# A two-block transformer step on one core: forget-gate weights on VectorE, last outputs in turn, final scaling on two engines

## The chip, the cores and the metric

The kernel runs on one core of a Trainium2 chip. A core has TensorE (PE, matrix products), VectorE (DVE), ScalarE (ACT), GpSimd (POOL) and the queues that issue transfers, here SP's. The metric is the device time of one execution in microseconds (us), lower is better.

## The reference, cut to what matters

The reference sends one sequence of 256 tokens of width 1024 through two blocks. Three places matter here. In the second block's mixer, half of the heads are forgetting attention: a per-head gate, summed along the sequence, is added to the scores.

```python
log_f = jax.nn.log_sigmoid((f_logit + b_forget)).transpose(0, 2, 1)
c = jnp.cumsum(log_f, axis=-1)
s = einsum('bhqd,bhkd->bhqk', qi, k) * scale + cq[..., None] - c[:, :, None, :]
```

The second block ends with a layer of 16,384 small experts. For each token some experts get a gate, all others none; the output is the gated gelu of the token with the experts' first matrix, times their second matrix, and a last norm follows.

```python
a = gates * jax.nn.gelu(xt @ u.T)      # gates are zero but for the chosen experts
h = h + a @ v
out = h * lax.rsqrt(jnp.mean(h * h, axis=-1, keepdims=True) + 1e-6) * norm_final_g
```

## The kernel before

Every weight comes from memory in units of 128x1024 (512 KB). `unit` splits a unit into a high part (`whi`, ScalarE, line 206) and a low part (`wlo`, DVE, line 209, or POOL for a share of the columns that `pool_k` sets, line 211). A product is three matmuls: high by high, low by high, high by low (`mm3`, lines 231 to 233). `take` and `wtile` hand out units and make up to two ahead.

Work that is not the main stream of products is written as generators. `spawn(gen, rate)` puts one on a list; `tick(w)` adds rate x w to each generator's account and calls it once for each whole number. `linear` makes two column tiles of 128 a group, and calls `tick(0.5)` behind each half of a group, so there are two half-ticks a group. `drain` runs what is left to its end. The instructions then stand on each engine's queue in an order that a scheduler derives from the program's order and from what is ready; each engine takes its queue in order.

The forget gate. `fox_c` makes the summed gate `u` for eight heads (8 partitions, 256 columns). `lh` (the tile `selh`, 8 heads x 256 columns, partitions 0 to 7 and 64 to 71) holds selectors which are multiplied by 8 u, so that a product with `rh` adds the gate to the scores. `fox_c` runs between two linears of the mixer. Behind it attention over the first half of the heads is spawned at rate 2.05 (`attention`, without gate: `scores` line 1360, `soft` lines 1369 to 1377, `turn` line 1383, `weigh`), and a linear of six groups follows; then `drain`, and the attention that reads `lh` (line 1364) is spawned.

The experts. `GT` holds 128x256 values for each of 128 rows of experts. A linear of 64 groups makes the products with the first matrix, and `evu` applies the gelu (lines 1446 to 1450). Meanwhile `wstep` builds the gates of four tokens a call from two comparisons (lines 1460, 1461) and a scaling (line 1463); the call after, `place` multiplies them out (eight matmuls, line 1470) and multiplies or copies them into all rows of `GT` that are done (lines 1473, 1475). The products with the second matrix start only with `GT` complete: for each pair `i` of rows, `split` makes `ah` and `al` (lines 332, 333), and 24 matmuls (line 1539) add to four accumulators `acc[t][c]`, two halves of 128 tokens by two blocks of 512 columns.

The tail (lines 1541 to 1554). Each accumulator is added to the residual, squared and summed on ScalarE, the root and reciprocal give a factor for each token, and one DVE instruction for each block multiplies by it and by the gain `gf`. Four transfers on SP's queue write the blocks.

Of the kernel before, what the change touches and what calls it, by code (L numbers as in the profile page):

```python
# [8 lines left out]
FT = mybir.dt.float32  # L9
# [4 lines left out]
AF = mybir.ActivationFunctionType  # L14
OP = mybir.AluOpType
# [3 lines left out]
P = 128  # L19
S = 256  # L20
# [142 lines left out]
class Kernel:  # L163
# [1162 lines left out]
    def fox_c(self, psum, pd, ps, r2):  # L1326
        nc = self.nc
        V, SC = nc.vector, nc.scalar
        t = lambda nm, shape: pd.tile(shape, FT, name=nm)
        z, u = t("fz", [8, S]), t("fu", [8, S])  # L1330
        V.tensor_tensor(z, ps[0:8, :], r2[0:8, :], op=OP.mult)
        V.tensor_scalar(z, z, self.v("b_forget")[0:8], None, op0=OP.add)
        SC.activation(u, z, AF.Abs)
        SC.activation(u, u, AF.Exp, scale=-1.0)
        SC.activation(u, u, AF.Ln, bias=1.0)
        V.tensor_scalar(z, z, 0.0, None, op0=OP.min)
        V.tensor_tensor(z, z, u, op=OP.subtract)
        V.tensor_tensor_scan(u, self.ones[0:8, 0:1].to_broadcast([8, S]), z, 0.0, op0=OP.mult, op1=OP.add)
        lh, rh, w = self.selh, t("frh", [P, S]), t("fw", [P, S])
        nc.gpsimd.memset(rh, 1.0)  # L1340
        for b in (0, 64):
            c = w[b:b + 8]
            V.tensor_scalar(c, u, 8.0, None, op0=OP.mult)
            nc.gpsimd.tensor_tensor(lh[b:b + 8], lh[b:b + 8], c[:, None, :].to_broadcast([8, 8, S]), op=OP.mult)
            V.tensor_scalar(rh[b + 32:b + 40, :], u, -8.0, None, op0=OP.mult)
        self.fox = (lh, rh)

    def attention(self, psum, pd, q, k, vt, amask, fox, oh, ol):
        nc = self.nc
# [60 lines left out]
    def peer(self):  # L1410
        nc, tc = self.nc, self.tc
        V, SC, G, T = nc.vector, nc.scalar, nc.gpsimd, nc.tensor
        x = self.xres
        with ExitStack() as es:
            pk = es.enter_context(tc.tile_pool(name="pk", bufs=1))
            it = {n: pk.tile([P, S], FT, name="t" + n) for n in ("i", "j", "g")}
            GT = pk.tile([P, P, S], FT, name="GT")
            with ExitStack() as e2:
# [36 lines left out]
                def build(t0):  # L1455
                    oj = pw.tile([P, 4, P], FT, name="oj")
                    om = pw.tile([P, 4, P], FT, name="om")
                    oe = wide[2 + t0 // 4 % 2].rearrange("p a (b c) -> p (a b) c", b=2)
                    z = slice(t0, t0 + 4)
                    V.tensor_tensor(oe, io4, it["i"][:, z, None].to_broadcast([P, 4, P]), op=OP.is_equal)  # L1460
                    V.tensor_tensor(oj, io4, it["j"][:, z, None].to_broadcast([P, 4, P]), op=OP.is_equal)
                    for j in range(4):
                        SC.activation(om[:, j, :], oe[:, j, :], AF.Copy, scale=it["g"][:, t0 + j:t0 + j + 1])  # L1463
                    return t0, oj, om

                def place(t0, oj, om):
                    i1 = st["u"]
                    wps = psum.tile([P, 4, P], FT, name="ax")
                    for j in range(4):
                        T.matmul(wps[:, j, :], oj[:, j, :], om[:, j, :], start=True, stop=True)  # L1470
                    z = slice(t0, t0 + 4)
                    if i1:
                        V.tensor_tensor(Gv[:, z, :i1], Gv[:, z, :i1], wps[:, :, :i1], op=OP.mult)
                    if i1 < P:
                        SC.activation(Gv[:, z, i1:], wps[:, :, i1:], AF.Copy)
                    st["n"] = t0 + 4

                def wstep():
                    q = []
                    for t0 in range(0, S, 4):  # L1480
                        if len(q) == 1:
                            place(*q.pop(0))
                        q.append(build(t0))
                        yield
                    for p in q:
                        place(*p)
                        yield

                def start_w():
                    for _ in top():  # L1490
                        yield
                    self.pool_k = 0
                    self.spawn(wstep(), 1.65)

                self.pool_k = 8

                def evq(n, ps):
                    SC.activation(qh[:, n:n + 2, :], ps, AF.Copy)
                    st["q"] = n + 2

                self.spawn(start_w(), 1.6, "top", pin=PIN)
                self.linear(psum, hh, hl, 16, 8, evq, outer=True)
                for k in range(0, 8, 2):
                    SC.activation(hh[:, k:k + 2, :], hn[:, k:k + 2, :], AF.Copy)
                    (G if k % 4 else V).tensor_tensor(hl[:, k:k + 2, :], hn[:, k:k + 2, :], hh[:, k:k + 2, :].bitcast(FT),  # L1505
                                                     op=OP.subtract)
# [6 lines left out]
                acc = [[psum.tile([P, 512], FT, name="ax") for _ in range(2)] for _ in range(2)]  # L1513
                pv = po
                flat = lambda k: GT[:, k:k + 8, :].rearrange("p a b -> p (a b)").rearrange("p (t d) -> p t d", t=2)
                xt, o, sq = flat(0), flat(8), flat(16)
                gf = GT[:, 24:28, :].rearrange("p a b -> p (a b)")

                def turn(t, c):
                    tp = psum.tile([P, 4, P], FT, name="ax")  # L1520
                    for k in range(4):
                        T.transpose(tp[:, k, :], x[:, 4 * c + k, t * P:(t + 1) * P], self.ident)
                    SC.activation(xt[:, t, c * 512:(c + 1) * 512], tp.rearrange("p a b -> p (a b)"), AF.Copy)

                for i in range(0, P, 2):
                    ah = pv.tile([P, 2, S], FR, name="ah")
                    al = pv.tile([P, 2, S], FR, name="al")
                    self.split(GT[:, i:i + 2, :], ah, al)
                    if i == 32:
                        nc.sync.dma_start(gf, self.A["gf"])  # L1530
                    if 32 < i <= 40:
                        turn(*divmod(i // 2 - 17, 2))
                    for u in range(2):
                        wh, wl = (w.rearrange("p a b -> p (a b)") for w in self.take(2))
                        for t in range(2):
                            z = slice(t * P, (t + 1) * P)
                            for n, (a, w) in enumerate(((ah, wh), (al, wh), (ah, wl))):
                                for c in range(2):
                                    T.matmul(acc[t][c], a[:, u, z], w[:, c * 512:(c + 1) * 512],  # L1539
                                             start=i + u == 0 and n == 0, stop=i + u == P - 1 and n == 2)  # L1540
                self.warm_sqrt(GT[:, P - 1, 0:1])
                ss = pv.tile([P, 2, 2], FT, name="ss")
                for t in range(2):
                    r = self.r1[:, t:t + 1]
                    for c in range(2):
                        z = slice(c * 512, (c + 1) * 512)
                        V.tensor_tensor(o[:, t, z], xt[:, t, z], acc[t][c], op=OP.add)
                        SC.activation(sq[:, t, z], o[:, t, z], AF.Square, accum_out=ss[:, t, c:c + 1])
                    V.tensor_tensor(r, ss[:, t, 0:1], ss[:, t, 1:2], op=OP.add)
                    self.rsqrt(r, r, 1.0 / D, 0)  # L1550
                    for c in range(2):
                        z = slice(c * 512, (c + 1) * 512)
                        V.scalar_tensor_tensor(o[:, t, z], o[:, t, z], r, gf[:, z], op0=OP.mult, op1=OP.mult)  # L1553
                        nc.sync.dma_start(self.out[:, t, z], o[:, t, z])

    def topk(self, psum, qh, keys, scr, it, st):
        nc = self.nc
# [124 lines left out]
```

## Time and profile before

| | |
|---|---|
| Median of 3 runs | 1574.6 us (1574.18 to 1577.16) |
| Time of the profiled execution | 1572.57 us |
| Its span, first to last instruction | 1570.8 us |
| Mean granted TensorE clock | 0.986 of full |
| Busy: PE, DVE, ACT, POOL | 1515.3, 1132.9, 837.0, 345.7 us |

The span is what the trace holds; the profiled execution's time is 1.8 us longer. Busy times are sums over stages with different limits.

### The profile page before, as it was taken

Reading aid. Unit: us, or ns where it says so; the run is one execution under the profiler, and the core shown is the slowest. Engines: PE = TensorE matmul, PEld = TensorE weight load, DVE = VectorE, ACT = ScalarE, POOL = GpSimd, SP = SyncE. Lnnn points to the kernel's source line nnn. Section 1 sums busy time; section 2 is a strip of 40 time slices with the busy share of each in tenths; the row PEclk is TensorE's granted clock in tenths of the full one; section 3 lists DMA queues with packets and bytes.
Section 4 is the critical chain, followed back from the end, with each engine's and each line's share of the span. In section 5 each row is a group of like instructions: output and inputs, shape, how many; then the busy total and the mean of one; then the engine's idle time right before and its main releaser. Section 6 shows DMA issues by size and latency. Waiting matters only on the chain.

```text
span 1570.8 us, 28981 instructions
## 1 busy us (share of the span) xinstructions
PE 1515.3 (96%) x11494; PEld 1412.3 (90%) x11494; DVE 1132.9 (72%) x1801; ACT 837.0 (53%) x1399; POOL 345.7 (22%) x303
## 2 busy tenths in 40 slices
PE   6898999999999989999999999999999999999997
PEld 5897889999999989999999999999998888888886
DVE  8789975887645676667688967888997555555554
ACT  4563334756644455545455457777765445444543
POOL 7514644335400120025791600000000000000000
PEclk9899999999999999999999999999999999999999
DMA  9455457476565644546555554444454666666663
GB/s 365 155 156 168 162 181 223 147 255 202 178 188 185 195 128 135 148 148 219 158 175 189 162 188 147 149 141 155 137 157 151 194 207 187 191 195 193 193 196 121
DMA packets 75448, 279.67 MB, mean 178 GB/s; under 512 B 8368, under 2 KB 9008, under 8 KB 73648
## 3 DMA queue, kind: packets, MB, share of 16 engines
q1 hardware_dynamic: 75312, 277.82, 55.9%
q8 instruction: 90, 1.47, 0.4%
q14 instruction: 46, 0.38, 0.1%
HBM read 275.69 MB, written 2.10 MB: 177 GB/s over the span
## 4 chain that ended last, share of the span: by engine, by line
PE 46%; DVE 2%; POOL 1%; issue 1%; ACT 0%; DVEq 0%; ACTq 0%
PE ax L1539 22%; PE mm L233 7%; PE mm L232 7%; PE mm L231 7%; PE ax L1470 4%; POOL wlo L211 1%; POOL GT L1604 0%; DVE GT L1636 0%; DVE wlo L209 0%; DVE GT L1634 0%; PE ax L1577 0%; DVE GT L1553 0%; ACT whi L206 0%; DVE GT L1614 0%; DVE GT L1615 0%
## 5 line engine op out<-in xcount | busy, mean ns | idle before, releaser
L206 ACT ACTIVATE whi<-raw 128x1024 fp32r<-128x1024 f32 x453 | 478.9, 1058 | 549.7 <-PE mm L232 199.0
L209 DVE TENSOR_TENSOR wlo<-raw,whi 128x1024 fp32r<-128x1024 f32 (+2 forms) x413 | 496.6, 1204 | 267.0 <-ACT whi L206 266.3
L231 PE MATMUL mm<-hh,whi 128*128 128x256 f32 x1816 | 524.8, 289 | 3.7 <-ACT gate L581 2.5
L233 PE MATMUL mm<-hh,wlo 128*128 128x256 f32 x1816 | 515.5, 284 | 3.1 <-DVE wlo L209 2.3
L232 PE MATMUL mm<-hl,whi 128*128 128x256 f32 x1816 | 512.7, 282 | 1.1 <-DVE hl L1505 0.7
L231 PEld LDWEIGHTS mm<-hh,whi 128*128 128x128 f32 x1816 | 344.9, 190 | 10.3 <-issue 5.2
L233 PEld LDWEIGHTS mm<-hh,wlo 128*128 128x128 f32 x1816 | 345.5, 190 | 5.0 <-DVE wlo L209 2.7
L232 PEld LDWEIGHTS mm<-hl,whi 128*128 128x128 f32 x1816 | 346.2, 191 | 2.9 <-issue 1.4
L211 POOL TENSOR_TENSOR wlo<-raw,whi 128x256 fp32r<-128x256 f32 (+2 forms) x112 | 187.4, 1679 | 161.0 <-ACT whi L206 105.0
L1539 PE MATMUL ax<-whi,ah 128*128 128x512 f32 x512 | 158.7, 391 | 3.9 <-ACT ah L332 3.9
L1539 PE MATMUL ax<-whi,al 128*128 128x512 f32 x512 | 158.4, 391 | 0.0
L1539 PE MATMUL ax<-wlo,ah 128*128 128x512 f32 x512 | 158.2, 390 | 0.0
L1539 PEld LDWEIGHTS ax<-whi,ah 128*128 128x128 f32 x512 | 96.0, 188 | 23.9 <-ACT ah L332 4.1
L1539 PEld LDWEIGHTS ax<-whi,al 128*128 128x128 f32 x512 | 96.5, 189 | 20.4 <-DVE al L333 0.4
L1539 PEld LDWEIGHTS ax<-wlo,ah 128*128 128x128 f32 x512 | 96.5, 188 | 20.1
L1463 ACT ACTIVATE om<-xres,tg 128x128 f32<-128x128 f32 x256 | 84.9, 392 | 1.0 <-DVE xres L1460 1.0
L233 PE MATMUL ax<-hh,wlo 128*128 128x258 f32 x256 | 73.0, 285 | 1.7 <-DVE wlo L209 1.6
L231 PE MATMUL mm<-fh,whi 128*128 128x256 f32 x256 | 73.0, 285 | 0.0
L233 PE MATMUL mm<-fh,wlo 128*128 128x256 f32 x256 | 72.9, 285 | 0.0
L232 PE MATMUL mm<-fl,whi 128*128 128x256 f32 x256 | 72.9, 285 | 0.0
L231 PE MATMUL ax<-hh,whi 128*128 128x258 f32 x256 | 72.6, 284 | 0.0
L232 PE MATMUL ax<-hl,whi 128*128 128x258 f32 x256 | 72.2, 282 | 0.0
(531 smaller groups left out, 2377.6 us busy)
## 6 DMA issues: line engine op xcount, KB each, us to landing
raw<-in_wts SPq DMA_DIRECT2D x453, 512.0 KB, 3.6
raw<-in_ada SPq DMA_DIRECT2D x24, 512.0 KB, 4.2
araw<-in_ada SPq DMA_DIRECT2D x8, 1024.0 KB, 7.9
w0r<-in_w SPq DMA_DIRECT2D x8, 576.0 KB, 8.9
araw<-in_ada SPq DMA_DIRECT2D x8, 512.0 KB, 4.9
x<-in_x SPq DMA_DIRECT2D x1, 1024.0 KB, 5.0
mb<-in_x SPq DMA_DIRECT2D x2, 512.0 KB, 5.0
selh<-in_att SPq DMA_DIRECT2D x1, 1024.0 KB, 5.9
```

The source lines that it names most:

```text
L206: nc.scalar.activation(hi, raw, AF.Copy)
L209: nc.vector.tensor_tensor(lo[:, :c], raw[:, :c], hi[:, :c].bitcast(FT), op=OP.subtract)
L211: nc.gpsimd.tensor_tensor(lo[:, c:], raw[:, c:], hi[:, c:].bitcast(FT), op=OP.subtract)
L231: mm(ps, wh, xh, start=start, stop=False, **kw)
L232: mm(ps, wh, xl, start=False, stop=False, **kw)
L233: mm(ps, wl, xh, start=False, stop=stop, **kw)
L1463: SC.activation(om[:, j, :], oe[:, j, :], AF.Copy, scale=it["g"][:, t0 + j:t0 + j + 1])
L1470: T.matmul(wps[:, j, :], oj[:, j, :], om[:, j, :], start=True, stop=True)
L1539: T.matmul(acc[t][c], a[:, u, z], w[:, c * 512:(c + 1) * 512], start=i + u == 0 and n == 0, stop=i + u == P - 1 and n == 2)
```

## The change

Three edits. In `fox_c` the two POOL multiplies of 8x2048 elements become a generator of eight DVE multiplies of 8x512, spawned at rate 0.8. `wstep` is spawned at 1.75 in place of 1.65. At the end, the table load for the square root moves from behind the loop into pair 64; the last pair takes both its units first and ends the four accumulators one after another; the gain is multiplied in ahead of the factor, into a place of its own, and the factor is then applied by DVE for one block and by ScalarE for the other.

```diff
@@ fox_c @@
             V.tensor_scalar(c, u, 8.0, None, op0=OP.mult)
-            nc.gpsimd.tensor_tensor(lh[b:b + 8], lh[b:b + 8], c[:, None, :].to_broadcast([8, 8, S]), op=OP.mult)
             V.tensor_scalar(rh[b + 32:b + 40, :], u, -8.0, None, op0=OP.mult)
         self.fox = (lh, rh)
+
+        def weights():
+            for h in range(0, 8, 2):
+                yield
+                for b in (0, 64):
+                    z, c = lh[b:b + 8, h:h + 2], w[b:b + 8]
+                    V.tensor_tensor(z, z, c[:, None, :].to_broadcast([8, 2, S]), op=OP.mult)
+
+        self.spawn(weights(), 0.8)
@@ start_w @@
-                    self.spawn(wstep(), 1.65)
+                    self.spawn(wstep(), 1.75)
@@ the last loop @@
-                xt, o, sq = flat(0), flat(8), flat(16)
+                xt, o, sq, og = flat(0), flat(8), flat(16), flat(28)
...
+                    if i == 64:
+                        self.warm_sqrt(ah[:, 0, 0:1].bitcast(FT))
+                    if i < P - 2:
...
+                    else:
+                        us = [[w.rearrange("p a b -> p (a b)") for w in self.take(k)] for k in (1, 0)]
                         for t in range(2):
                             z = slice(t * P, (t + 1) * P)
-                            for n, (a, w) in enumerate(((ah, wh), (al, wh), (ah, wl))):
-                                for c in range(2):
-                                    T.matmul(acc[t][c], a[:, u, z], w[:, c * 512:(c + 1) * 512],
-                                             start=i + u == 0 and n == 0, stop=i + u == P - 1 and n == 2)
-                self.warm_sqrt(GT[:, P - 1, 0:1])
+                            for c in range(2):
+                                for u, (wh, wl) in enumerate(us):
+                                    for n, (a, w) in enumerate(((ah, wh), (al, wh), (ah, wl))):
+                                        T.matmul(acc[t][c], a[:, u, z], w[:, c * 512:(c + 1) * 512],
+                                                 start=False, stop=u == 1 and n == 2)
@@ the tail @@
                         V.tensor_tensor(o[:, t, z], xt[:, t, z], acc[t][c], op=OP.add)
                         SC.activation(sq[:, t, z], o[:, t, z], AF.Square, accum_out=ss[:, t, c:c + 1])
+                        V.tensor_tensor(og[:, t, z], o[:, t, z], gf[:, z], op=OP.mult)
...
-                        V.scalar_tensor_tensor(o[:, t, z], o[:, t, z], r, gf[:, z], op0=OP.mult, op1=OP.mult)
-                        nc.sync.dma_start(self.out[:, t, z], o[:, t, z])
+                        if c:
+                            SC.activation(og[:, t, z], og[:, t, z], AF.Copy, scale=r)
+                        else:
+                            V.tensor_scalar(og[:, t, z], og[:, t, z], r, None, op0=OP.mult)
+                        nc.sync.dma_start(self.out[:, t, z], og[:, t, z])
```

In all pairs but the last the 24 matmuls stay as they were.

## Rows read from the trace of the kernel before

**Rows 1.** TensorE's waits over the span: total, times, longest, in us.
```profile
PE ax L1383 <- DVE sc L1377: 5.6, 2, 4.2
...
PE ax L1539 <- ACT ah L332: 3.9, 1, 3.9
```

**Rows 2.** Busy time by stretch; (x) instructions; then granted clock, DMA share, GB/s.
```profile
580.00:600.00 20.00, 18.80 (x142) 17.90 (x143) 16.81 (x38) 11.99 (x29) 0.00 (x0) 0.86 0.54 158
...
880.00:900.00 20.00, 18.28 (x151) 17.79 (x150) 19.79 (x30) 10.55 (x13) 8.75 (x4) 1.00 0.51 160
...
1180.00:1200.00 20.00, 20.00 (x173) 20.00 (x173) 18.67 (x23) 13.91 (x36) 0.00 (x0) 1.00 0.53 156
1200.00:1220.00 20.00, 16.12 (x89) 13.74 (x88) 11.93 (x12) 9.04 (x15) 0.00 (x0) 0.91 0.49 160
...
1380.00:1400.00 20.00, 20.00 (x90) 16.57 (x89) 11.09 (x11) 9.73 (x12) 0.00 (x0) 1.00 0.64 197
```

**Rows 3.** Instructions in order of time, POOL and DVE: start, duration, idle before.
```profile
569.14 4.69 POOL L1344 TENSOR_TENSOR selh<-selh,fw 8x2048 f32<-8x2048 f32 x1 [18.70 <-DVE fw L1343]
574.13 4.53 POOL L1344 TENSOR_TENSOR selh<-selh,fw 8x2048 f32<-8x2048 f32 x1 [0.30 <-DVE fw L1343]
...
568.79 0.27 DVE L1343 TENSOR_SCALAR fw<-fu 8x256 f32<-8x256 f32 x1
...
569.39 4.59 DVE L1343 TENSOR_SCALAR fw<-fu 8x256 f32<-8x256 f32 x1
...
575.47 3.54 DVE L1377 TENSOR_SCALAR sc<-sc,mx 128x128 f32<-128x128 f32 x2
```

**Rows 4.** Instructions in order of time, TensorE, 573 to 595.
```profile
573.71 0.93 PE L1360 MATMUL ax<-ka,qa 64*128 64x128 f32 x8
578.80 0.95 PE L1383 MATMUL ax<-main,sc 128*128 128x128 f32 x3 [4.16 <-DVE sc L1377]
...
581.73 0.56 PE L231 MATMUL mm<-hh,whi 128*128 128x256 f32 x1
...
585.66 0.28 PE L231 MATMUL mm<-hh,whi 128*128 128x256 f32 x1
...
593.13 0.93 PE L1360 MATMUL ax<-ka,qa 64*128 64x128 f32 x8
...
594.62 0.36 PE L231 MATMUL mm<-hh,whi 128*128 128x256 f32 x1
```

**Rows 5.** Instructions in order of time, all engines, 1204 to 1215.
```profile
1204.78 1.05 PE L1470 MATMUL ax<-om,oj 128*128 128x128 f32 x8
...
1205.93 0.58 ACT L1449 ACTIVATE xres<-mm 128x504 f32<-128x504 f32 x1
...
1206.53 1.28 ACT L440 ACT_TABLE_LOAD   x1
...
1207.73 1.26 DVE L1473 TENSOR_TENSOR GT<-GT,ax 128x512 f32<-128x512 f32 x1
...
1209.71 0.80 PE L1539 MATMUL ax<-whi,ah 128*128 128x512 f32 x2 [3.88 <-ACT ah L332]
...
1214.30 0.62 PE L1539 MATMUL ax<-whi,ah 128*128 128x512 f32 x2
```

**Rows 6.** The chain that ended last, from 1540: start, time, what.
```profile
1539.83 21.77 PE ax L1539 x96
...
1561.63 0.70 DVE GT L1547
...
1562.35 1.33 ACT GT L1548 x4
...
1564.10 1.42 DVE GT L1553 x2
...
1565.63 0.75 DVE GT L1553
1566.38 0.66 DVEq L1677
```

More of the change, by code (lines that the diff above doesn't have):

```diff
@@ L1532, in peer @@
                         turn(*divmod(i // 2 - 17, 2))
-                    for u in range(2):
-                        wh, wl = (w.rearrange("p a b -> p (a b)") for w in self.take(2))
+                    if i == 64:
+                        self.warm_sqrt(ah[:, 0, 0:1].bitcast(FT))
+                    if i < P - 2:
+                        for u in range(2):
+                            wh, wl = (w.rearrange("p a b -> p (a b)") for w in self.take(2))
+                            for t in range(2):
+                                z = slice(t * P, (t + 1) * P)
+                                for n, (a, w) in enumerate(((ah, wh), (al, wh), (ah, wl))):
+                                    for c in range(2):
+                                        T.matmul(acc[t][c], a[:, u, z], w[:, c * 512:(c + 1) * 512],
+                                                 start=i + u == 0 and n == 0, stop=False)
+                    else:
+                        us = [[w.rearrange("p a b -> p (a b)") for w in self.take(k)] for k in (1, 0)]
                         for t in range(2):
                             z = slice(t * P, (t + 1) * P)
-                            for n, (a, w) in enumerate(((ah, wh), (al, wh), (ah, wl))):
-                                for c in range(2):
-                                    T.matmul(acc[t][c], a[:, u, z], w[:, c * 512:(c + 1) * 512],
-                                             start=i + u == 0 and n == 0, stop=i + u == P - 1 and n == 2)
-                self.warm_sqrt(GT[:, P - 1, 0:1])
+                            for c in range(2):
+                                for u, (wh, wl) in enumerate(us):
+                                    for n, (a, w) in enumerate(((ah, wh), (al, wh), (ah, wl))):
+                                        T.matmul(acc[t][c], a[:, u, z], w[:, c * 512:(c + 1) * 512],
+                                                 start=False, stop=u == 1 and n == 2)
                 ss = pv.tile([P, 2, 2], FT, name="ss")
```

## Prediction

> **What bounds the kernel now.** I read the stretches first (busy time of each engine in windows of 20 us), because the share over the whole span hides where TensorE is not the limit. In most of the second half TensorE is busy for 20.00 of 20 us with a granted clock of 1.00, as in 1180 to 1200 [rows 2]; there a change of another engine is worth nothing. Two windows fall out: 580 to 600 (18.80, clock 0.86) and 1200 to 1220 (16.12, clock 0.91) [rows 2]. The list of TensorE's waits names the same two places: line 1383 waits for line 1377 twice, 5.6 us together, and line 1539 waits once for line 332, 3.9 us [rows 1]. Then I read both places in order of time, and last the chain that ended last, for the tail. The change touches these three places, so the forecast is three terms.
>
> **Place one, the forget-gate weights.** Two POOL multiplies of 8x2048 elements run from 569.14 and 574.13, 4.69 and 4.53 us [rows 3]. In the same time a DVE tensor_scalar of 8x256 takes 4.59 us from 569.39 (to 573.98, when the first multiply has ended at 573.83), and two of line 1377 take 3.54 us from 575.47 (to 579.01, the second multiply ends at 578.66) [rows 3]. Both DVE instructions end about when POOL lets go, so I read them as held by POOL. TensorE is behind them: eight score matmuls start at 573.71, the transposes only at 578.80, after 4.16 us of idle time, and the next projection matmul at 581.73 [rows 4]. One cycle later the same two steps take 594.62 - 593.13 = 1.49 us [rows 4]; here 581.73 - 573.71 = 8.02, so 6.5 us are lost. Then 18 matmuls need 585.66 - 581.73 = 3.93 us [rows 4], 0.218 each, where 173 fit into 20.00 us of an undisturbed window, 0.116 each [rows 2]: about half rate, the lower of the two levels, after that idle time. That is 18 x 0.102 = 1.8 us more. Place one costs 8.3 us.
>
> The change takes both POOL multiplies away. DVE gets eight multiplies of 8x512 instead, by the nearest row, a DVE add of 512 columns, 0.70 us each [rows 6]: 5.6 us. They are issued late and apart: at 0.8 per tick and six ticks in that linear, the generator is called at half-ticks 3, 5 (or 6), 8 and 10; the first call only yields, three give a pair each (1.4 us), and the last pair falls into the drain. So no pair stands in front of the first softmax, which is what TensorE waited for. Behind a pair wait the next wlo subtraction and the softmax of a later cycle. DVE is idle for 3.19 us even of 580 to 600 [rows 2], which still holds work delayed by POOL. I cost the eight multiplies at nothing; without that idle time a pair would delay TensorE by its 1.4 us, three pairs by 4.2.
>
> What is late next at place one is the DVE work itself: without POOL, the held tensor_scalar gives back 4.59 less the 0.27 us of the same instruction before it, 4.3, and the pair of line 1377 gives back 3.54 less twice 0.27, 3.0, so 7.3 together, against 6.5 us that TensorE lost [rows 3, 4]. That leaves under 1 us of slack, so I keep 0.8 us of wait and take 7.5 us of 8.3 as saved; ends: 8.3, and 0 if the held DVE instructions had another cause.
>
> **Place two, the end of the expert stage.** wstep needs 65 calls (64 builds, and the last placement). At 1.65 a half-tick adds 0.825, so call 65 comes at half-tick 79; at 1.75 it adds 0.875 and call 65 comes at half-tick 75. The trace has the last eight placement matmuls at 1204.78, behind the last linear matmul [rows 5]: half-tick 79 is the last of the stage. The new last placement thus comes two groups earlier, inside the stream.
>
> Behind the old last placement stands a chain: its DVE multiply from 1207.73 for 1.26 us, then ah, then the first matmul of line 1539 at 1209.71, after 3.88 us of idle time [rows 5]. The next twelve matmuls need 1214.30 - 1209.71 = 4.59 us [rows 5]; the chain's last 96 need 21.77, 0.227 each [rows 6], so twelve should need 2.72: 1.9 us lost at the lower clock. Place two costs 5.8 us. The eight placement matmuls are only moved. With the placement done two groups earlier, the first two rows of GT are final and ah and al of the first pair can be made under the last groups. I take 5.3 us as saved, keeping 0.5 for whatever ScalarE still has in front of ah. From below: ah behind the last gelu (it ends at 1206.51 [rows 5]) plus about 0.7 for ah gives a first matmul at 1207.2, a saving of 2.5 with the clock lost all the same.
>
> The faster rate itself costs DVE nothing on the path, but its cover is thin. DVE is busy for 18.67 of 20 us in 1180 to 1200 [rows 2]; if all of it grew by 1.75/1.65 it would be 19.8. So DVE stays under TensorE, by 1% at least. If that cover is gone over the last nine groups, some 65 us, each per cent too much costs 0.65 us; I keep 0 to 2 us and take 0.
>
> **Moved table load.** warm_sqrt goes from behind the loop into pair 64. The trace has a load of 1.28 us, from 1206.53, before ah, which ends at 1207.81, while ah's input is ready only at 1207.73 + 1.26 = 1208.99 [rows 5]; so it binds nothing now. In the loop ScalarE is busy 9.73 of 20 us [rows 2], so in a pair of 24 x 0.227 = 5.4 us it is idle 2.8; the load and its one-column activation fit in. Cost 0. [...]
>
> **Place three, the tail.** The last matmul ends at 1561.60, the last scaling at 1567.04, 5.44 us later [rows 6]. The old chain: add 0.70, two squares in a row 1.33, root and reciprocal 0.41, then four scalings by line 1553 with a reciprocal between them, from 1564.10 on [rows 6]. With the accumulators ending in turn, a quarter of 24 x 0.227 = 1.36 us apart, only the last add and one square (0.67) follow the last matmul, then the sum (0.2, estimated as half of root and reciprocal, another one-column operation), root and reciprocal 0.41, and one scaling, on DVE and ScalarE side by side. For it the 0.75 us of the old one [rows 6] is the nearest row. Sum: 0.70 + 0.67 + 0.2 + 0.41 + 0.75 = 2.7; with the hand-overs of 0.02, 2.8. Saved: 2.6. The gain-weight multiply (0.70 again) of the last block lies beside its square; but that of the block before may stand ahead of the last add on DVE, and two output transfers now become ready together on SP's one queue. I take 2.0; ends 0.9 (both delays) and 2.7. Reading both units of the last pair at once wants the last wlo some 2 us earlier; TensorE has no wait anywhere in this loop but its first [rows 1], and units are made ahead. Cost 0.
>
> **Sum.** 7.5 + 5.3 + 2.0 = 14.8 us. The profiled execution took 1572.57 us (span 1570.8), so it would take 1557.8; the median of the runs shown is 2.0 us above that execution, 1574.6, so I forecast 1559.8 for the median.
>
> **Rivals.**
> 1. A new wait at place one: the softmax is late again because DVE's order puts other work before it (a wlo subtraction, or a weights pair). For it: under 1 us of slack. Against: the pairs are issued later. It leaves some 4 us of the wait and the low clock behind it, 5.5 in all: 1565.
> 2. At place two ah stands behind the gelu: saving 2.5 instead of 5.3, so 1562.6. For it: in the old order ah is ScalarE's last. Against: there it could not be earlier, its input was not ready.
> 3. Slower: DVE becomes the bound at 1.75. Place: 1100 to 1190, where its load is highest. If TensorE starved there and fell to the lower clock, a group of 48 matmuls would cost 48 x 0.102 = 4.9 us more, so three eat the gain of 14.8 and the point from which it decides is the fourth; five give 1559.8 + 24.5 = 1584. For it: the high DVE share. Against: the 1% of cover, and that 1.7 us of idle time in 880 to 900 left the clock at 1.00 [rows 2]. [...]
> 4. The change doesn't do what it says at place one: the held DVE instructions had another cause, and the wait stays. Then 5.3 + 2.0 are saved: 1567.3.
>
> **Chances and range.** Forecast 0.68, rival 1 0.10, rival 2 0.11, rival 3 0.04, rival 4 0.05, nothing at all 0.02. The likeliest's own range is 1557 to 1563.5: all gains at their upper ends (8.3 + 5.8 + 2.7 = 16.8) give 1557.8, less some spread of the runs (1574.18 to 1577.16). Taking in rivals 1 and 2 and most of rival 4: 1557 to 1567. By more than 0.2% (3.1 us, about what a measurement of this kernel can tell from no change) faster: all cases but rival 3 and nothing, 0.94; same 0.03; slower 0.03.
>
> **What would show it.** Right: no POOL work at 569 to 579, DVE's tensor_scalars of 8x256 at 0.3 us, TensorE at 20.00 with clock 1.00 where now 580 to 600 stands; no wait of line 1539 for ah at its start, the last placement two groups before it; from the last matmul to the last scaling 3.4 us in place of 5.44. Wrong: a wait of line 1383 for line 1377 that stays over 2 us; waits of line 1470 or 233 for DVE between 930 and 1200; the last add behind another DVE multiply by over 0.7 us.

## The result, and the profile after

The changed kernel took 1557.83 us (median of 4 runs, 1556.54 to 1561.31), the kernel before 1574.39 (median of 4, 1572.68 to 1577.16). The ratio is 0.9899, with a 95% interval of 0.9887 to 0.991: 1.0% faster, 16.6 us by the medians. The forecast was 1559.8 with a range of 1557 to 1567. The profiled execution took 1556.54 us with a span of 1554.8, against 1572.57 and 1570.8 before, so the profiled spans differ by 16.0 us.

To see where these 16.0 us come from, I cut both spans at the same five instructions: the first DVE operation on the forget gate (fz), the first score matmul that reads its weights, the first placement matmul of the expert stage, and the first and the last matmul of the last loop. The differences of start times in the trace, in us:

| stretch | before | after | difference | forecast |
|---|---|---|---|---|
| start to fz (untouched) | 560.95 | 560.45 | -0.50 | 0 |
| fz to first score matmul (place one) | 60.45 | 52.20 | -8.25 | -7.5 |
| to first placement matmul (untouched) | 310.67 | 310.55 | -0.12 | 0 |
| to first matmul of the last loop (place two, wait) | 277.64 | 273.60 | -4.04 | -3.4 |
| to its last matmul (place two, clock) | 351.72 | 349.84 | -1.88 | -1.9 |
| to the end (tail) | 9.33 | 8.13 | -1.20 | -2.0 |

All three places became shorter, the first two by more than was forecast, the tail by less; the untouched stretches moved by 0.5 us and 0.1. In the rows of stretches (columns as in [rows 2]) the two windows that had fallen out are full, and in the expert stage the window with the highest DVE share still leaves TensorE at 20.00:

```profile
580.00:600.00 20.00, 20.00 (x170) 18.18 (x169) 19.01 (x42) 12.44 (x31) 0.00 (x0) 1.00 0.51 157
...
1100.00:1120.00 20.00, 20.00 (x173) 20.00 (x173) 19.58 (x24) 14.60 (x38) 0.00 (x0) 1.00 0.43 133
...
1200.00:1220.00 20.00, 20.00 (x90) 16.57 (x89) 10.97 (x11) 9.85 (x12) 0.00 (x0) 1.00 0.79 249
```

TensorE is at 20.00 and the granted clock at 1.00 where [rows 2] had 18.80 and 0.86, and 16.12 and 0.91. Neither wait of [rows 1] is in the list of waits of the changed kernel.

**Place one.** DVE in order of time, the counterpart of [rows 3]:

```profile
568.88 0.28 DVE L1343 TENSOR_SCALAR fw<-fu 8x256 f32<-8x256 f32 x1
...
570.64 0.54 DVE L1385 TENSOR_SCALAR sc<-sc,mx 128x128 f32<-128x128 f32 x2
...
572.75 0.16 DVE L1383 RECIPROCAL mx<-mx 128x2 f32<-128x2 f32 x1
572.82 0.66 DVE L1352 TENSOR_TENSOR selh<-selh,fw 8x512 f32<-8x512 f32 x1
573.41 0.53 DVE L1385 TENSOR_SCALAR sc<-sc,mx 128x128 f32<-128x128 f32 x2
```

The second scaling of the gate takes 0.28 us in place of 4.59, the pair of softmax scalings 0.54 in place of 3.54. Yet the first weights multiply does not come late: it stands at 572.82, between the reciprocal and the scalings of the second softmax; in front of the first softmax's scalings (570.64) there is none, as forecast. TensorE, the counterpart of [rows 4], does not notice:

```profile
573.22 0.93 PE L1368 MATMUL ax<-ka,qa 64*128 64x128 f32 x8
574.08 0.88 PE L1391 MATMUL ax<-main,sc 128*128 128x128 f32 x6
574.71 0.36 PE L231 MATMUL mm<-hh,whi 128*128 128x256 f32 x1
```

From the score matmuls to the next projection it takes 574.71 - 573.22 = 1.49 us, the undisturbed step of [rows 4]. The second softmax is done at 573.94, and the six transposes start at 574.08, behind the score matmuls. As three belong to each softmax ([rows 4] has them in threes) and six take 574.71 - 574.08 = 0.63 us, the second softmax is needed, as an estimate, at 574.4: the multiply had some 0.4 us of room.

**Place two.** DVE, ScalarE and TensorE at the end of the expert stage, the counterpart of [rows 5]:

```profile
1187.45 1.32 DVE L1481 TENSOR_TENSOR GT<-GT,ax 128x496 f32<-128x496 f32 x1
...
1188.88 0.62 ACT L332 ACTIVATE ah<-GT 128x512 fp32r<-128x512 f32 x1
...
1192.19 0.58 ACT L1457 ACTIVATE xres<-mm 128x512 f32<-128x512 f32 x1
...
1196.68 0.28 PE L233 MATMUL mm<-hh,wlo 128*128 128x256 f32 x1
1196.80 0.63 PE L1550 MATMUL ax<-whi,ah 128*128 128x512 f32 x2
```

The last placement's multiply ends at 1188.77, 8.0 us ahead of the loop; ah is made in front of the last gelu, not behind it; the first matmul of the loop follows the last linear one without a gap.

**The tail.** DVE and ScalarE around the last add (line 1566), then the chain that ended last, the counterpart of [rows 6]:

```profile
1546.43 0.69 DVE L1568 TENSOR_TENSOR GT<-GT 128x512 f32<-128x512 f32 x1
1547.06 0.69 DVE L1566 TENSOR_TENSOR GT<-GT,ax 128x512 f32<-128x512 f32 x1
...
1548.39 0.48 DVE L1576 TENSOR_SCALAR GT<-GT,r 128x512 f32<-128x512 f32 x1
1548.41 0.71 ACT L1574 ACTIVATE GT<-GT,r 128x512 f32<-128x512 f32 x1
1548.79 0.15 DVE L1569 TENSOR_TENSOR r<-ss 128x1 f32<-128x1 f32 x1
...
1549.03 0.28 ACT L378 ACTIVATE r<-r,eps 128x1 f32<-128x1 f32 x1
```

```profile
1547.78 0.72 ACT GT L1567 x2
1548.51 0.61 ACT GT L1574
1549.12 0.19 ACT r L378
...
1549.53 0.72 ACT GT L1574
```

The last matmul starts at 1546.64, the last add 0.42 us behind it, as the gain multiply of the block before ends; the sum (1548.79), root, reciprocal and two scalings side by side follow. In front of the sum and the root stand the scalings of the first half of the tokens, on DVE (1548.39) and on ScalarE (1548.41). The last scaling ends at 1550.25: 3.6 us. Before, the same two were 1561.43 and 1567.04, 5.6 us. (The forecast's 5.44 counted from 1561.60, which in the trace is the end of the next-to-last matmul; from the end of the same matmul, 1546.80, it is 3.46 now.) So 2.0 us are saved up to there, but only 1.2 arrive at the end. The four output transfers of 256 KB, issued in pairs in the changed kernel and apart in the one before, show why. The time from issue to landing, for the changed kernel first, then for the kernel before, last for the last output of the kernel before alone:

```profile
L1577 SPq DMA_DIRECT2D out<-GT x4: 332/384/450, 1548.9 to 1550.4; - x4
...
DMA to landing us min/median/max: 2.4/2.9/3.2
```

```profile
L1554 SPq DMA_DIRECT2D out<-GT x4: 332/338/343, 1564.9 to 1567.1; - x4
...
DMA to landing us min/median/max: 2.4/2.5/2.7
```

```profile
L1554 SPq DMA_DIRECT2D out<-GT x1: 332/332/332, 1567.1 to 1567.1; - x1
...
DMA to landing us min/median/max: 2.5/2.5/2.5
```

The last output now leaves within 0.4 us of the third and lands 3.20 us after its issue; before, it left 0.7 us after the third and landed after 2.55. (The 2.7 of the kernel before is its second output's.) That is 0.65 us; another 0.14 is the last issue, which stands 0.17 us behind its scaling in place of 0.03. Together they are the 0.8 us that do not arrive.

### The profile page after: what moved, and what is told of

Read it like the earlier page. It is cut to its first block, busy times and chain, and to the rows that moved or that the text cites. A ratio compares the mean times of both kernels' runs of the same rounds, so it can differ in the third digit from the quotient of the medians.

```text
span 1554.8 us, 28988 instructions
## 1 busy us (share of the span) xinstructions
PE 1510.4 (97%) x11494; PEld 1409.9 (91%) x11494; DVE 1130.5 (73%) x1811; ACT 839.1 (54%) x1400; POOL 335.9 (22%) x301
## 4 chain that ended last, share of the span: by engine, by line
PE 46%; DVE 2%; POOL 1%; issue 1%; ACT 0%; DVEq 0%
PE ax L1550 22%; PE mm L233 7%; PE mm L232 7%; PE mm L231 7%; PE ax L1478 4%; POOL wlo L211 1%; POOL GT L1627 0%; DVE GT L1659 0%; DVE GT L1566 0%; DVE GT L1657 0%; DVE wlo L209 0%; PE ax L1600 0%; DVE GT L1568 0%; DVE GT L1637 0%; DVE GT L1638 0%
## 5 line engine op out<-in xcount | busy, mean ns | idle before, releaser
L209 DVE TENSOR_TENSOR wlo<-raw,whi 128x1024 fp32r<-128x1024 f32 (+2 forms) x413 | 496.3, 1204 | 265.0 <-ACT whi L206 264.4
L1481 DVE TENSOR_TENSOR GT<-GT,ax 128x208 f32<-128x208 f32 (+31 forms) x64 | 62.4, 974 | 16.1 <-PE ax L1478 15.9
```

Source lines behind the costliest of these rows:

```text
L209: nc.vector.tensor_tensor(lo[:, :c], raw[:, :c], hi[:, :c].bitcast(FT), op=OP.subtract)
```

## The experiments

### The three parts alone

`a_fox` has the kernel before with the forget-gate part only, `b_rate` with the rate only, `c_tail` with the edits of the last loop and the tail only.

```
a_fox   -   nc.gpsimd.tensor_tensor(lh[b:b + 8], lh[b:b + 8], c..., op=OP.mult)
        +   def weights(): ...
        +   self.spawn(weights(), 0.8)
b_rate  -   self.spawn(wstep(), 1.65)
        +   self.spawn(wstep(), 1.75)
c_tail  +   the last pair ordered by accumulator; og = o * gf; scaling on DVE and ACT; warm_sqrt at i == 64
```

> The kernel before with the forget-gate edit alone. Theory (three separate places, place one worth 8.3 us by its trace): span 1570.8 - 8.3 = 1562.5, no wait of the transposes for the softmax near 574, clock 1.00 in 560 to 620; the wait of 3.9 us at the start of the last loop and the lower clock behind it stay. Rival (the rate or the tail edit did part of it, or the gain at place one is given back at the end of the expert stage, whose call positions are unchanged): span above 1565.

> The kernel before with the rate 1.75 alone. Theory: place two is worth 5.8 to 6.0 us: span 1564.9, no wait of the first matmul of the last loop, last placement two groups before it. Rival (DVE, busier at this rate, makes TensorE wait before 1190, and the gain is smaller): waits of lines 233 or 1470 for DVE and a span above 1566.

> The kernel before with the edits of the last loop and the tail alone. Theory: from the last matmul to the last scaling 3.4 us in place of 5.4, but the last outputs land some 0.7 us later after their issue than before, so the span is 1.3 us shorter, 1569.5. Rival (the landing in the changed kernel was chance): span 2.0 us shorter or more, 1568.8.

| | median us | ratio to before, 95% | fz to scores | placements to loop | loop | tail |
|---|---|---|---|---|---|---|
| before | 1573.7 | | 60.5 | 277.6 | 351.7 | 9.3 |
| a_fox | 1566.78 | 0.9955 (0.9939 to 0.9972) | 52.2 | 277.6 | 351.5 | 9.3 |
| b_rate | 1570.7 | 0.9979 (0.9969 to 0.9988) | 60.8 | 273.6 | 349.8 | 9.3 |
| c_tail | 1572.71 | 0.9995 (0.9985 to 1.0005) | 60.3 | 277.6 | 351.6 | 8.2 |

In the stretches each part moves its own place, and the others behind fz by 0.4 us at most: -8.3, -5.9 (-4.0 and -1.9) and -1.2, which makes the 15.4 that the three places give in the whole change. The medians say less: 6.9 + 3.0 + 1.0 = 10.9, against 16.6 for the whole. In the profiled executions the difference lies ahead of every edit: fz begins at 564.0, 565.9 and 564.6 us in those of the three, at 560.9 and 560.5 in those of before and after. That the other executions lose their time in the same place is likely, but they have no trace. So the median of one part is no measure of its price here, and c_tail's alone is inconclusive; the stretches decide. For the same reason the spans that were expected of the three parts and of the next two runs are missed by 2.7 to 5.3 us; less the later begin of fz, all five come within 0.4 us of the value expected or into its range. All later stretches of this section are read in the same way.

### Is it POOL that holds DVE, or where the multiplies stand

`d_poolbg` leaves the eight multiplies in the background but gives them to POOL. `e_inline` leaves them on DVE but issues all eight at once, in front of the first softmax. Both are edits of the changed kernel.

```
d_poolbg  -   V.tensor_tensor(z, z, c[:, None, :]..., op=OP.mult)
          +   nc.gpsimd.tensor_tensor(z, z, c[:, None, :]..., op=OP.mult)
e_inline  -   self.spawn(weights(), 0.8)
          +   for _ in weights(): pass
```

> The changed kernel with the eight background multiplies on POOL in place of DVE. Theory (POOL's reads hold a DVE tensor_scalar until the running POOL instruction ends): POOL does them one after another from 569 on, some 1.2 us each; single DVE tensor_scalars are stretched by up to 1.2 us each but not by 4, so TensorE waits 0 to 3 us: span 1555 to 1558. Rival (the DVE instruction of before was slow by itself, not through POOL): no DVE instruction is stretched, span 1554.8 or less, as DVE has less to do.

> The changed kernel with the eight DVE multiplies issued at once in fox_c, not as a background part. Theory (what counts is what stands in front of the first softmax on DVE): 5 us of multiplies come ahead of it, TensorE waits 4 to 5 us for line 1386 (the softmax's scaling) near 574 and runs some matmuls at the lower clock: span 1554.8 + 4.5 to 6.5 = 1559.3 to 1561.3. Rival (the gain is only from leaving POOL, the background part is of no matter): span 1554.8 to 1555.5.

d_poolbg took 1563.31 us (ratio 0.9922, 0.9903 to 0.994), e_inline 1566.5 (0.9947, 0.9931 to 0.9964); from fz to the scores they need 54.7 and 58.4 us, 2.5 and 6.2 more than the changed kernel. So the move to DVE and the place in the background are each worth something. In d_poolbg POOL and DVE overlap; first POOL in order of time:

```profile
573.77 1.39 POOL L1352 TENSOR_TENSOR selh<-selh,fw 8x512 f32<-8x512 f32 x1 [18.69 <-DVE fw L1343]
575.45 12.26 POOL L1352 TENSOR_TENSOR selh<-selh,fw 8x512 f32<-8x512 f32 x7 [0.30 <-DVE fw L1343]
```

The multiplies by their line (duration in ns, shortest, median and longest), and DVE in the same stretch:

```profile
L1352 POOL TENSOR_TENSOR selh<-selh,fw x8: 1260/1400/2167, 573.8 to 585.5; 8x512 f32<-8x512 f32 x8
```

```profile
573.41 0.27 DVE L1343 TENSOR_SCALAR fw<-fu 8x256 f32<-8x256 f32 x1
...
574.02 1.29 DVE L1343 TENSOR_SCALAR fw<-fu 8x256 f32<-8x256 f32 x1
...
575.65 0.69 DVE L1278 TENSOR_TENSOR qb<-mm,r 128x512 f32<-128x512 f32 x1
...
576.79 1.57 DVE L1385 TENSOR_SCALAR sc<-sc,mx 128x128 f32<-128x128 f32 x2
...
578.80 1.82 DVE L209 TENSOR_TENSOR wlo<-raw,whi 128x1024 fp32r<-128x1024 f32 x1
...
582.02 2.30 DVE L209 TENSOR_TENSOR wlo<-raw,whi 128x1024 fp32r<-128x1024 f32 x1
```

The same gate scaling takes 0.27 us with POOL idle, 1.29 behind a POOL multiply that ends at 575.16 (the scaling ends 0.15 us later, at 575.31), and 4.59 behind the long one of [rows 3], where it ends 0.15 us later too. Its time follows the length of the POOL instruction (1.39 and 4.69 us), so I read it as held until POOL lets go; in both traces the POOL instruction had begun 0.25 us earlier. The pair of softmax scalings is held as well, for 1.57 us in place of 0.54. Not every DVE instruction is: the product of line 1278 takes 0.69 us with POOL at work, as it does without (0.69 in the changed kernel). Two wlo subtractions stretch too, from 1.22 to 1.82 and 2.30, and a POOL multiply takes up to 2.17 us where the shortest takes 1.26: both sides are longer there. What sets the instructions that are held apart from the one that is not, no run shows.

The two runs also show what becomes of the wait on TensorE. First d_poolbg, then e_inline (DVE, then TensorE):

```profile
581.99 0.61 PE L1391 MATMUL ax<-main,sc 128*128 128x128 f32 x3 [2.24 <-DVE sc L1385]
...
582.55 0.28 PE L232 MATMUL mm<-hl,whi 128*128 128x256 f32 x1
```

```profile
573.48 5.54 DVE L1352 TENSOR_TENSOR selh<-selh,fw 8x512 f32<-8x512 f32 x8
...
580.19 0.54 DVE L1386 TENSOR_SCALAR sc<-sc,mx 128x128 f32<-128x128 f32 x2
```

```profile
580.52 0.95 PE L1392 MATMUL ax<-main,sc 128*128 128x128 f32 x3 [2.42 <-DVE sc L1386]
...
581.48 0.41 PE L232 MATMUL mm<-hl,whi 128*128 128x256 f32 x1
...
583.03 0.41 PE L232 MATMUL mm<-hl,whi 128*128 128x256 f32 x1
```

In e_inline the eight multiplies take 5.54 us and push the softmax behind them: TensorE waits 2.42 us (4 to 5 were expected), and its matmuls then follow each other at 0.21 us, not 0.12, until 587.5. The granted clock of 580 to 600 is 0.83. In d_poolbg the wait is 2.24 us and the matmuls behind it keep 0.12; its clock is 1.00. The 6.2 us of e_inline are the 2.4 of wait, another 0.54 at 582.43, and some 30 matmuls that take 0.1 longer each at the lower clock. This is what rival 1 of the prediction describes.

A third try, `i_poolafter`, was to keep the two long POOL multiplies of the kernel before but to put them behind all four gate scalings.

```
i_poolafter  (on the kernel before)
        for b in (0, 64):  V.tensor_scalar(w[b:b + 8], ...); V.tensor_scalar(rh..., ...)
    +   for b in (64, 0):  nc.gpsimd.tensor_tensor(lh[b:b + 8], ..., op=OP.mult)
```

> The kernel before with both POOL multiplies behind all four tensor_scalars of fox_c (in the other order of partitions, so that the first waits for the second tensor_scalar). Theory (held by POOL): the second tensor_scalar of 8x256 takes 0.3 us in place of 4.59, and what is held now is the softmax's pair of line 1377, until one or both multiplies have ended; TensorE waits still 4 us or more there, span 1570 to 1573. Rival (that tensor_scalar is slow by itself): it still takes over 4 us.

It took 1576.13 us (1.0004, 0.9993 to 1.0014). It does not answer its question: in the trace a POOL multiply still begins at 571.54, right behind the first gate scaling at 571.19, and the second gate scaling takes 4.59 us from 571.79. The order on the engines is not the one written down; the run repeats the kernel before.

### Does the higher rate bring DVE near the bound

`g_rate200` raises the rate further.

```
g_rate200  -   self.spawn(wstep(), 1.75)
           +   self.spawn(wstep(), 2.0)
```

> The changed kernel with wstep at 2.0. Theory (DVE is near its limit at 1.75 and over it at 2.0 late in the stage): the last placement comes some seven groups before the end, DVE is busy all of the time before it, TensorE waits for DVE there, 1 to 4 us in sum; span 1555.8 to 1558.8. Rival (there is cover enough, the stage is TensorE's at any of these rates): span 1554.8 within 0.5. A second rival (starved groups fall to the lower clock): granted clock under 0.97 in some window of 1050 to 1160, span over 1565.

It took 1559.9 us (0.9904, 0.9886 to 0.9923). Its stretch from the scores to the last loop is 584.19 us, the changed kernel's 584.15. One window, then the group of the placement multiplies (line, count, busy us, mean ns), and the same group in the changed kernel:

```profile
1120.00:1140.00 20.00, 20.00 (x173) 20.00 (x172) 19.88 (x25) 15.21 (x40) 0.00 (x0) 1.00 0.42 135
```

```profile
L1481 DVE TENSOR_TENSOR GT<-GT,ax 128x200 f32<-128x200 f32 (+31 forms) x64 | 59.2, 925 | 8.3 <-PE ax L1478 6.4 <-ACT whi L206 1.6
```

```profile
L1481 DVE TENSOR_TENSOR GT<-GT,ax 128x208 f32<-128x208 f32 (+31 forms) x64 | 62.4, 974 | 16.1 <-PE ax L1478 15.9
```

DVE at 19.88 of 20 still leaves TensorE at 20.00 and the clock at 1.00. The rate packs the same 64 multiplies closer, and as they come earlier they are narrower: 63.8 us in all before, 62.4 at 1.75, 59.2 at 2.0. So rival 3 does not occur even at 2.0, and neither does the wait of 1 to 4 us for DVE that was expected; 2.0 brings nothing, because nothing waited any more.

### Where 0.8 us of the tail went

Four runs take the tail apart. `h_ogpool` gives the two gain multiplies of the first half of the tokens to POOL, so that DVE has less to do in front of the last scalings; `k_actdma` issues the outputs that ScalarE scaled from ScalarE's queue; `m_order` has the new order of the last pair with the old scaling; `n_scale` has the new scaling with the old order. All are edits of the changed kernel.

```
h_ogpool  -   V.tensor_tensor(og[:, t, z], o[:, t, z], gf[:, z], op=OP.mult)
          +   (V if t else G).tensor_tensor(og[:, t, z], o[:, t, z], gf[:, z], op=OP.mult)
k_actdma  -   nc.sync.dma_start(self.out[:, t, z], og[:, t, z])
          +   (nc.scalar if c else nc.sync).dma_start(self.out[:, t, z], og[:, t, z])
m_order   -   V.tensor_tensor(og...) ; SC.activation(og..., scale=r) ; V.tensor_scalar(og..., r, ...)
          +   V.scalar_tensor_tensor(o[:, t, z], o[:, t, z], r, gf[:, z], ...)
n_scale   -   if i < P - 2:
          +   if i < P:        (and stop at the last matmul of the loop)
```

> The changed kernel with the gain multiply of the first token half on POOL, which is idle there. Theory (in the tail DVE is the queue that orders things: the first half's scaling waits behind adds and multiplies): the first half's outputs are issued about 1 us earlier, the last two land without others beside them, span 0.5 to 1.0 us shorter, 1553.8 to 1554.3. Rival (POOL's reads hold DVE's adds or scalings, or the last chain does not hang on it): span 1554.8 or longer.

> The changed kernel with the two output transfers of the second column block issued on ScalarE's queue, not SP's. Theory (the last two outputs take longer after their issue, 3.2 us for the last against 2.5 before, because their transfers lie side by side with the two ahead of them): from the start of the last matmul to the end stays 8.2 us within 0.15. Rival (they wait for each other's issue on SP's queue, 0.4 us each): 0.2 to 0.5 us shorter, 7.7 to 8.0.

> The changed kernel with the scaling of before (one DVE instruction for each block applies factor and gain, no gain multiply ahead, nothing on ScalarE); the order of the last pair and the moved table load stay. Theory (the order of the accumulators is what shortens the tail; the gain multiplies fill DVE and the four outputs come out closer together): last scaling ends 3.5 to 3.8 us after the last matmul, outputs land 2.5 us after their issue, start of last matmul to end 7.7 to 8.2 us against 8.2. Rival (the split scaling is worth its 0.7 us): 8.8 us or more.

> The changed kernel with the last pair's 24 matmuls in the old order; gain multiply ahead and split scaling stay. Theory (the order is what shortens the tail): the adds of all four blocks fall behind the last matmuls and DVE has four more multiplies there, start of last matmul to end 8.8 to 9.6 us, no gain against 9.4 of the kernel before. Rival (the split scaling is what shortens it): 8.4 us or less.

| | median us | ratio, 95% | last matmul's start to last scaling's end | from there to the end | landing, median and longest |
|---|---|---|---|---|---|
| before | 1574.88 | | 5.6 | 3.7 | 2.5, 2.7 |
| after | 1557.83 | 0.9899 (0.9887 to 0.991) | 3.6 | 4.5 | 2.9, 3.2 |
| h_ogpool | 1558.23 | 0.9894 (0.9875 to 0.9914) | 3.6 | 4.5 | 2.9, 3.2 |
| k_actdma | 1560.23 | 0.9914 (0.9892 to 0.9935) | 3.7 | 4.5 | SP 2.6, ScalarE 3.2; 3.3 |
| m_order | 1560.35 | 0.9912 (0.9891 to 0.9933) | 4.7 | 3.7 | 2.5, 2.6 |
| n_scale | 1561.58 | 0.992 (0.9899 to 0.994) | 5.6 | 4.1 | 2.6, 2.9 |

Each ratio is the recorded one, against the executions of the kernel before that belong to that run, and not a quotient of the medians shown. The intervals overlap; again the stretches are what is read. In h_ogpool the multiplies run on POOL, but DVE's order stays, and nothing is gained:

```profile
1547.34 0.69 DVE L1566 TENSOR_TENSOR GT<-GT,ax 128x512 f32<-128x512 f32 x1
1547.95 0.16 DVE L379 RECIPROCAL r<-r 128x1 f32<-128x1 f32 x1
1548.07 0.69 DVE L1568 TENSOR_TENSOR GT<-GT 128x512 f32<-128x512 f32 x1
```

The reciprocal of the first half still stands behind the last add, and its scaling behind the last gain multiply (at 1548.67); the outputs leave as in the changed kernel, the first 2.3 us after the start of the last matmul in both. The last add starts 0.42 us after that matmul in both, and 0.43 after it in m_order, which has no gain multiply: the gain multiplies, one of my two possible delays, cost nothing here.

In k_actdma the last output leaves right behind its scaling (1552.35 against 1552.32), past SP's queue, and the end does not come sooner:

```profile
out<-GT SPq DMA_DIRECT2D x2, 256.0 KB, 2.6
out<-GT ACTq DMA_DIRECT2D x2, 256.0 KB, 3.2
```

So it is not SP's order of issue: what the last output gains by leaving earlier, 0.14 us, it loses by landing later (3.31 us after its issue). In m_order the outputs are spaced by the old scalings, 0.7 us apart and more, and they land as before:

```profile
1551.15 1.41 DVE L1572 SCALAR_TENSOR_TENSOR GT<-GT,r 128x512 f32<-128x512 f32 x2
...
1553.20 1.42 DVE L1572 SCALAR_TENSOR_TENSOR GT<-GT,r 128x512 f32<-128x512 f32 x2
```

Transfers that leave 0.4 us apart land in up to 3.2 us from one queue and 3.3 from two, those that leave 0.7 us apart in 2.5 to 2.7: an output close behind another took longer. n_scale shows the two parts of it. It has the changed kernel's scalings and sources, but 1.9 us between its pairs in place of 0.8; there the second of each pair lands after 2.85 and 2.82 us, and the first, with nothing issued just ahead of it, after 2.41 and 2.38. So the 3.20 of the changed kernel's last output is, as an estimate, 2.4 for an output alone, 0.4 for the one just ahead of it and 0.4 for the pair ahead. That is how part of the split's gain is given back. The order alone brings 5.6 - 4.7 = 0.9 us of work and no later landing. The split alone brings nothing (5.6), and its end comes 0.4 us later than in the kernel before: in the old order the two last gain multiplies stand on DVE in front of the sum that everything waits for,

```profile
1552.05 1.29 DVE L1568 TENSOR_TENSOR GT<-GT 128x512 f32<-128x512 f32 x2
...
1553.25 0.15 DVE L1569 TENSOR_TENSOR r<-ss 128x1 f32<-128x1 f32 x1
```

where the squares had been read out at 1553.06. With the order the split saves another 4.7 - 3.6 = 1.1 us of work, of which 4.5 - 3.7 = 0.8 is lost on the way out; 0.3 us arrive. Neither expectation was quite met: from the start of the last matmul to the end m_order takes 8.4 us, between the theory's 8.2 and the rival's 8.8, and n_scale 9.7, just above the 9.6 that the theory allowed.

## Why the prediction was right, and where its terms were off

**The reading.** The forecast took the windows and waits of TensorE as the whole price, and the three places in them as the three terms. That held: the untouched stretch between places one and two moved by 0.1 us, and each part alone moved its own place by what it moved in the whole. Rival 4 (another cause of the held DVE instructions) falls with d_poolbg, in which the same instructions are held again for as long as the shorter POOL instructions last (the gate scaling for 1.29 us beside 1.39), and with a_fox, which gives the whole gain of place one. That POOL held DVE is shown by these runs, not only argued.

**Place one: 7.5 forecast, 8.3 measured.** The mechanism was right. The mis-sized term is the 0.8 us of wait that I kept for DVE's own work; no wait is left, so the upper end of the range was the true value. That no multiply stands in front of the first softmax came true. The step that the pairs come late was wrong: the first multiply runs in the first cycle, ahead of the second softmax's scalings. It costs nothing because of some 0.4 us of room, not because of its place. e_inline shows what lies beyond the room: 6.2 us. The chance of 0.10 for rival 1 was for a real danger.

**Place two: 5.3 forecast, 5.9 measured.** The placement came two groups earlier as worked out, and the low clock at the loop's start was worth 1.9 as forecast. The mis-sized term is the 0.5 kept for ScalarE: ah is made 7.9 us before the loop and in front of the gelu, so rival 2 falls.

**DVE's load at the higher rate.** I scaled all of DVE's work by 1.75/1.65. The windows grew by less in 1160 to 1180 (18.85 before, 19.21 after) and by more in 1100 to 1120 (17.98 to 19.58), as the same multiplies moved to an earlier time and became narrower (the changed kernel also reaches the stage 8.9 us earlier, so its windows show slightly later work). The scaling was wrong, the conclusion (no cost) right; g_rate200 shows that there was room to 19.88.

**The moved table load: 0 forecast.** The load of 1.28 us now stands at 1368.69, the activation that follows it at 1369.98. No wait of line 1550 is in the list. The next activation begins right behind the 1.28 us, as in the kernel before (load at 1206.53, activation at 1207.85).

**The tail: 2.0 forecast, 1.2 measured.** Two steps were off. The chain was to save 2.6 us up to the last scaling; 2.0 was taken, which leaves 0.6 for two possible delays, a gain multiply ahead of the last add and outputs that become ready together. Up to the last scaling only 2.0 are saved, though the gain multiply cost nothing. The count began at the end of the next-to-last matmul, and the new last add waits for the last one, 0.26 us later. And the scalings "on DVE and ScalarE side by side" were counted once, while those of the first half stand on both engines just ahead of the sum and the root: from the last square's end (1548.51) to the root's start (1549.03) it takes 0.52 us, where the sum was to take 0.2. This is read from the order of the instructions; no run takes the scalings of the first half away. Then the outputs cost 0.8 (0.65 in landing, 0.14 in issue), more than the 0.6 that was left for both delays. That the 2.0 agrees with what is saved up to the last scaling is luck.

**The sum.** Measured by stretches: 8.3 + 5.9 + 1.2 = 15.4, against 14.8. The two reserves that weren't needed (0.8 and 0.5; what came above the forecast is 1.4) outweigh the tail (0.8). The profiled span shrank by 0.6 more in stretches that the change does not touch. The median lies only 1.3 us above the profiled execution, where 2.0 had been taken over from three runs of the kernel before. These three make the 2.0 us between 1559.8 and 1557.83. That the profiled spans of before and after can be set against each other at all is partly luck: fz begins at 560.9 and 560.5 us in them, and up to 5 us later in the profiled executions of other kernels with the same work ahead of it.

## What to carry to other kernels

Where DVE instructions beside a POOL instruction take as long as POOL does (4.59 us beside 4.69 here), moving POOL's work to DVE can be a gain even though DVE is the busier engine (8.3 us here): price it by the DVE instructions that are held and by what waits for them, and spread the moved work so that none of it stands whole in front of the waiting engine. Keep a matmul loop's first operand ready before the stage ahead of it ends; the wait can be paid twice, once as idle time and once at the lower clock behind it (4.0 and 1.9 us here). In a tail, follow the chain up to the landing of the last output, since outputs that left close together landed later here (3.2 us against 2.5), and look at what the engines do for the blocks ahead of the last.

## What the runs showed of the hardware that was not expected

**The first 560 us differ between kernels that share them.** From the start to fz, profiled executions took 560.4 to 565.9 us, with the same work in that stretch: 560.9 before, 565.9 in b_rate, 560.5 after. From 100 to 300 us TensorE was busy for 186.46 us at a mean granted clock of 0.95 in the changed kernel, for 185.18 at 0.94 in c_tail. Runs of one kernel spread about as much (1556.54 to 1561.31 for the changed kernel), and each kernel has one profile here, so whether the shift belongs to the kernel or to the execution stays open. The executions without a trace speak for a share of the kernel: the ten of b_rate lie 3.0 us below the kernel before by the median and 3.4 by the fastest (1568.79 against 1572.22), where its place gave 5.9. The shift is the likely reason that the medians of the parts do not add up, while the stretches do.

**Two waits of nearly the same length went with different clocks.** At place one a wait of 2.24 us left the clock at 1.00 (d_poolbg), one of 2.42 us, with another of 0.54 us behind it, went with matmuls 0.21 us apart in place of 0.12 (e_inline). The low rate was there before the second wait: the matmul at 581.48 took 0.41 us, where the same one takes 0.28 in d_poolbg. Two runs do not make a rule, and what stands around the two waits differs as well; the price was 2.5 us in the one and 6.2 in the other.
